# Moving the cosine and sine tables of a fused encoder layer into its modulation steps

## The chip, the cores and the metric

One core of one Trainium2 chip runs the whole layer. The metric is the device time of one execution in microseconds (us), as the median of several runs; the profile is one execution taken by the hardware profiler.

## The reference, cut to what matters

Sequence length 1024, model width 1024, one layer, float32. The rotary part of the second attention group needs the cosine and the sine of 1024 positions times 32 frequencies:

```python
mod = jax.nn.silu(c) @ ada_w + ada_b
shift, scale, gate = jnp.split(mod, 3, axis=-1)
h = _rms_norm(x, norm_g) * (1.0 + scale[:, None, :]) + shift[:, None, :]
proj = h @ w_in
dq, dk, dv, cq, ckv, kr, g = jnp.split(proj, [int(v) for v in cuts], axis=-1)
...
inv_freq = ROPE_THETA ** (-jnp.arange(half, dtype=jnp.float32) / half)
ang = positions.astype(jnp.float32)[:, :, None] * inv_freq
cos, sin = jnp.cos(ang), jnp.sin(ang)
q_pe = _rope(q_pe, cos[:, :, None, :], sin[:, :, None, :])
k_pe = jnp.broadcast_to(_rope(kr, cos, sin)[:, :, None, :], (B, S, MLA_HEADS, MLA_ROPE_DIM))
...
out = (mixed * jax.nn.silu(g)) @ w_out
return x + gate[:, None, :] * out
```

`dq`, `dk`, `dv` feed a differential attention, `cq`, `ckv`, `kr` a latent attention (MLA); both are chunk-causal.

## The kernel before, in words

The program has three phases: `prologue`, `projections` and `mixing`. Only the first and the start of the second matter here.

Products of two float32 operands are made of three matrix products each (`mm3`, lines 63 to 65): both operands are split into a rounded part and a rest, `hTh` and `hTl` for the activations, `wh` and `wl` for the weights. A raw weight tile `wraw` of 128 rows is loaded by SyncE's queue, cast to `wh` on ScalarE (line 534), and `wl = wraw - wh` is made on GpSimd or on VectorE (line 535). There are five buffers for `wraw` and eight for each of `wh` and `wl`, so the tiles of the next unit of weights are taken in as those of the last are done with.

The prologue normalizes `x`, transposes it to `xT` (eight slices `k` of 128 of the model width, two halves `b` of 512 tokens each), and then runs **modulation steps**, one for each `k`, in an order that is written out by hand for TensorE, VectorE, ScalarE and GpSimd (`manual_schedule`). While TensorE multiplies slice `k` with the MLA columns of `w_in` (448 columns) for seven of the eight tiles of 128 tokens (`step`, lines 392 to 398), the step makes the operands of slice `k + 1`:

- TensorE forms a part of `silu(c) @ ada_w` (`gemv`, `gv`, line 322), ScalarE copies it (line 324), TensorE turns it into a column (`mod`, line 330), and this comes in the middle of TensorE's step.
- VectorE makes scale and shift of the slice from it (`ab_mod`, lines 332 to 334).
- `modulated` does for each half `b`: VectorE forms `h32` (line 374, shown as `h`), ScalarE `hTh` (line 375), VectorE `hTl` from both (line 377).
- `split` casts slice `k + 2` of the weights on ScalarE (`wh`) and makes `wl` on GpSimd; `load` fetches slice `k + 4`.

In the last step VectorE does `gain_products` (lines 140 to 149) in the place of a modulation. After the steps the pool `x`, which holds the input tiles, is closed, and the pool `tmp` takes its memory. From here on a scheduler sets the order of instructions on each engine. `mla_evac` copies the seven accumulators from PSUM to `lat` (line 602 on ScalarE, line 604 on VectorE). TensorE does the eighth token tile (`u1b`) and then the unit of 512 columns for the keys `dk` (the first `u` of lines 63 to 65 with 512 columns); its tiles of results take turns in the PSUM banks that the accumulators held, and are emptied by way of `sq`, `ss`, `r` and `xn` (line 561). `mla_latent` normalizes `lat`, and `mla_weights` splits the weights that MLA needs.

`rope_tables` stands after the first `mla_latent`. It loads the positions and the frequencies through GpSimd's queue (lines 160 and 161), and makes the tables `cc` (cosine) and `sc` (sine, with sign) with 29 operations on VectorE, nearly all on 128 x 256 elements and each on the result of the one before: the angle, its reduction to one turn, a series for the sine, a series for the cosine, and four copies into the tables (lines 234 and 235). Its scratch is taken from the stage buffers of `tmp` (the tile `scr`). The tables are first read when `mla_tile` rotates `kr` on GpSimd (`rope`, lines 645 to 648), in the first token tiles of the unit `dk`.

Of the kernel before, what the change touches and what calls it, by code (L numbers as in the profile page):

```python
# [17 lines left out]
P = 128  # L18
S = 1024
D = 1024  # L20
# [25 lines left out]
GAINS = 4  # L46


class Fused:
# [101 lines left out]
    def rope_tables(self):  # L151
# [16 lines left out]
        )  # L168
        n = buf()
        stt = v.scalar_tensor_tensor  # L170

        def reduce_turns(t):
            v.tensor_scalar(n, t, MAGIC, None, op0=ALU.add)
            v.tensor_scalar(n, n, -MAGIC, None, op0=ALU.add)
            v.tensor_tensor(t, t, n, op=ALU.subtract)

        if not self.general:

            v.tensor_scalar(n, ang, 1.0 / (2.0 * math.pi), MAGIC, op0=ALU.mult, op1=ALU.add)
            v.tensor_scalar(n, n, -MAGIC, None, op0=ALU.add)  # L180
            p1 = 6.28125
            p2 = 507.0 * 2.0 ** -18
            p3 = 2.0 * math.pi - p1 - p2
            for p in (p1, p2, p3):
                stt(ang, n, -p, ang, op0=ALU.mult, op1=ALU.add)
            v.tensor_scalar(ang, ang, -4.0, 4.0, op0=ALU.max, op1=ALU.min)
        else:
# [6 lines left out]
            v.tensor_copy(hi, ang)  # L194
            v.tensor_tensor(lo, ang, hi.bitcast(F32), op=ALU.subtract)
            limbs = []
# [6 lines left out]
            for limb in reversed(limbs):  # L203
                for part in (lo, hi.bitcast(F32)):
                    v.tensor_scalar(f, part, limb, None, op0=ALU.mult)
                    reduce_turns(f)
                    reduce_turns(f)
                    if first:
                        v.tensor_copy(tot, f)
                        first = False  # L210
                    else:
                        v.tensor_tensor(tot, tot, f, op=ALU.add)
                        reduce_turns(tot)
            v.tensor_scalar(ang, tot, 2.0 * math.pi, None, op0=ALU.mult)
            parts += [hi.bitcast(F32).rearrange("p t n -> p (t n)"), f.rearrange("p t n -> p (t n)")]

        y, sh, ch = n, buf(), buf()
        stt(y, ang, 0.25, ang, op0=ALU.mult, op1=ALU.mult)

        def series(out, first, last):  # L220

            v.tensor_scalar(out, y, (-1.0) ** (last // 2) / math.factorial(last), None, op0=ALU.mult)
            for d in range(last - 2, first, -2):
                stt(out, out, (-1.0) ** (d // 2) / math.factorial(d), y, op0=ALU.add, op1=ALU.mult)

        series(sh, 1, 13)
        stt(sh, sh, 1.0, ang, op0=ALU.add, op1=ALU.mult)
        series(ch, 0, 14)
        stt(ch, ch, 1.0, sh, op0=ALU.add, op1=ALU.mult)

        stt(sh, sh, -0.5, sh, op0=ALU.mult, op1=ALU.mult)
        for h in range(2):
            sl = slice(h * 32, h * 32 + 32)
            v.tensor_scalar(self.cc[:, :, sl], sh, 1.0, None, op0=ALU.add)
            v.tensor_scalar(self.sc[:, :, sl], ch, -1.0 if h == 0 else 1.0, None, op0=ALU.mult)


    def prologue(self):
# [176 lines left out]
        rows_r = xp.tile([P, 4, P], F32, name="rows_r")  # L415
        rbc = [xp.tile([P, 512], F32, name=f"rbc{b}") for b in range(2)]
        split = lambda k: self.split_rows(unit, raws.pop(k), True)
        with self.tc.manual_schedule(engines={E.PE, E.DVE, E.Activation, E.Pool}):
# [6 lines left out]
            squares(0)  # L425
            turned(0, 0, range(6))
            squares(1)
# [1045 lines left out]
```

## Time and profile before

| | us |
|---|---|
| median of 3 runs | 679.31 (675.96 to 681.81) |
| the profiled execution | 675.18 |
| its span, first to last instruction | 673.2 |
| TensorE busy | 636.0 |
| VectorE busy | 480.0 |
| ScalarE busy | 341.3 |
| GpSimd busy | 282.5 |

In what follows PE is TensorE's matrix products, DVE VectorE, ACT ScalarE, POOL GpSimd. A row of a timeline gives the start, the length, the engine, the line, the operation and `out<-in` by the program's names; in brackets stands how long the engine was idle before it and what ended that. TensorE's products overlap one another, so the distance from start to start is what one takes. Busy time says little on an engine that waits for others by turns; what counts is the wait that ends last.

### The profile page before, as it was taken

To read this page: it belongs to the slowest core of one execution; us is meant where nothing else is said; L and a number is where in the kernel's file an instruction comes from. 1 tells how busy PE (TensorE), PEld (TensorE's weight loads), DVE (VectorE), ACT (ScalarE), POOL (GpSimd) and SP (SyncE) were. 2 spreads that over 40 slices of the span, in tenths; PEclk is the share of its full clock that TensorE was granted. 3 is DMA by queue.
4 is the path that set the end of the run, shared out by engine and by line. 5 is a ranking of instruction groups with operands and counts; after the bars stand their busy time and mean duration, and the time that the engine had idled before them with its cause. 6 is when DMAs were issued, how large, how long until landed. Compare 5 with 4: busy or idle time off the path is not lost.

```text
span 673.2 us, 11178 instructions
## 1 busy us (share of the span) xinstructions
PE 636.0 (94%) x3579; PEld 538.7 (80%) x3579; DVE 480.0 (71%) x1296; ACT 341.3 (51%) x820; POOL 282.5 (42%) x376
## 2 busy tenths in 40 slices
PE   6899998999999999989999989997999899999996
PEld 4578886878888888877888878886988788888885
DVE  5855899699987554635876867989976466367654
ACT  4433663744565344345766766877775344236200
POOL 2022415483355135304443544558655225349400
PEclk9999999999999999999999998998999999999999
DMA  9984152598657455499556385493365944514223
GB/s 323 304 203 127 41 172 58 148 286 263 185 144 217 120 162 148 133 237 291 139 151 188 98 241 132 137 289 123 95 188 169 300 144 134 148 46 126 80 111 113
DMA packets 115140, 112.97 MB, mean 168 GB/s; under 512 B 7712, under 2 KB 86614, under 8 KB 115072
## 3 DMA queue, kind: packets, MB, share of 16 engines
q1 hardware_dynamic: 114784, 112.12, 57.4%
q8 instruction: 30, 0.49, 0.3%
q14 instruction: 38, 0.31, 0.2%
q0 software_dynamic: 288, 0.05, 0.1%
HBM read 77.51 MB, written 34.62 MB: 167 GB/s over the span
## 4 chain that ended last, share of the span: by engine, by line
PE 62%; DVE 14%; DMA 11%; issue 4%; ACT 3%; POOL 3%; SPq 2%; DVEq 0%; POOLq 0%; ACTq 0%
PE lg L953 8%; PE u L63 7%; PE u L65 7%; PE u L64 7%; PE o L65 4%; PE o L63 4%; PE o L64 4%; PE pt L1019 3%; DVE p L962 3%; DMA raw<-mk_d 2%; PE acc L64 2%; PE acc L65 2%; PE acc L63 2%; PE u L392 2%; DMA dk<-dk_d 2%
## 5 line engine op out<-in xcount | busy, mean ns | idle before, releaser
L972 ACT ACTIVATE p<-p,mx 128x128 f32<-128x128 f32 (+7 forms) x96 | 74.3, 775 | 35.4 <-DVE p L967 19.2
L63 PE MATMUL u<-wh,hTh 128*128 128x512 f32 x192 | 75.8, 398 | 3.3 <-DVE xn L561 2.6
L65 PE MATMUL u<-wh,hTl 128*128 128x512 f32 x192 | 76.3, 397 | 0.0
L64 PE MATMUL u<-wl,hTh 128*128 128x512 f32 x192 | 75.7, 394 | 0.0
L962 DVE TENSOR_SCALAR_CACHE_REDUCE p<-lg 128x512 f32<-128x512 f32 (+5 forms) x96 | 52.6, 563 | 13.3 <-PE pt L1019 4.5
L953 PE MATMUL lg<-dk,dq 128*128 128x512 f32 (+2 forms) x192 | 52.2, 368 | 5.6 <-DVE p L962 3.3
L535 POOL TENSOR_TENSOR wl<-wraw,wh 128x512 fp32r<-128x512 f32 (+1 forms) x20 | 26.5, 1329 | 65.4 <-ACT wh L534 60.7
L63 PE MATMUL u<-hTh,wh 128*128 128x512 f32 x128 | 51.5, 402 | 0.0
L65 PE MATMUL u<-hTh,wl 128*128 128x512 f32 x128 | 51.0, 399 | 0.0
L64 PE MATMUL u<-hTl,wh 128*128 128x512 f32 x128 | 50.5, 394 | 0.0
L1019 PE MATMUL pt<-ident_r,p 128*128 128x128 f32 x288 | 45.9, 276 | 3.4 <-DVE pTl L1021 1.7
L63 PEld LDWEIGHTS u<-wh,hTh 128*128 128x128 f32 x192 | 36.1, 188 | 10.6 <-DVE xn L561 3.3
L65 PEld LDWEIGHTS u<-wh,hTl 128*128 128x128 f32 x192 | 36.1, 188 | 7.2 <-issue 0.4
L64 PEld LDWEIGHTS u<-wl,hTh 128*128 128x128 f32 x192 | 36.1, 188 | 6.7
L953 PEld LDWEIGHTS lg<-dk,dq 128*128 128x128 f32 x192 | 31.4, 195 | 11.3 <-DVE p L962 6.1
L1021 DVE TENSOR_TENSOR pTl<-pt,pTh 128x512 fp32r<-128x512 f32 x48 | 32.9, 688 | 10.6 <-ACT pTh L1020 10.2
L1107 POOL TENSOR_SCALAR p<-p,sm 128x128 f32<-128x128 f32 (+7 forms) x32 | 25.7, 806 | 34.7 <-DVE sm L1106 34.1
L1052 DVE SCALAR_TENSOR_TENSOR p<-p,sm,p 128x128 f32<-128x128 f32 (+7 forms) x32 | 33.1, 1040 | 9.7 <-POOL p L1051 9.7
L1019 PEld LDWEIGHTS pt<-ident_r,p 128*128 128x128 f32 x288 | 34.2, 141 | 6.4 <-DVE p L1052 2.5
L1020 ACT CAST pTh<-pt 128x512 fp32r<-128x512 f32 x48 | 27.5, 581 | 21.0 <-PE pt L1019 20.6
L1051 POOL TENSOR_SCALAR p<-p,sm 128x128 f32<-128x128 f32 (+7 forms) x32 | 25.5, 797 | 27.6 <-DVE sm L1050 10.6
L953 PE MATMUL lg<-mkh,mq 128*128 128x512 f32 (+2 forms) x96 | 34.0, 365 | 0.7 <-ACT mq L877 0.7
(321 smaller groups left out, 1913.8 us busy)
## 6 DMA issues: line engine op xcount, KB each, us to landing
wraw<-in_w_in_dram SPq DMA_DIRECT2D x40, 256.0 KB, 3.4
ada<-in_ada_w_dram SPq DMA_DIRECT2D x32, 256.0 KB, 6.6
dq<-dq_d SPq DMA_DIRECT2D x16, 512.0 KB, 6.9
xt<-in_x_dram SPq DMA_DIRECT2D x8, 512.0 KB
dk_d<-st SPq DMA_DIRECT2D x16, 256.0 KB
adag<-in_ada_w_dram SPq DMA_DIRECT2D x16, 256.0 KB
dq_d<-st SPq DMA_DIRECT2D x16, 256.0 KB, 3.1
sg_d<-sgt SPq DMA_DIRECT2D x16, 256.0 KB, 4.7
```

Of the source, the lines that this page charges most:

```text
L63: t.matmul(out, wh, xh, start=start, stop=False)
L64: t.matmul(out, wh, xl, start=False, stop=False)
L65: t.matmul(out, wl, xh, start=False, stop=stop)
L535: (nc.gpsimd if pool else nc.vector).tensor_tensor(l, raw, h.bitcast(F32), op=ALU.subtract)
L953: self.last_mm = nc.tensor.matmul(lg[:, :w], q, k, start=j == 0, stop=j == len(ops) - 1 and not add)
L962: nc.vector.tensor_scalar(o[:, :m], lg[:, :m], 1.0, mx if c0 else None, op0=ALU.mult, op1=ALU.min, accum_out=mx)
L972: nc.scalar.activation(p, p, AF.Exp, bias=mx, scale=-1.0, accum_out=sm)
L1019: nc.tensor.transpose(t[:, j * P : j * P + P], ptiles[e[1]][:, e[0] * P : e[0] * P + P], self.ident)
L1020: nc.scalar.copy(h[:, lo:512], t[:, lo:512])
L1021: nc.vector.tensor_tensor(l[:, lo:512], t[:, lo:512], h[:, lo:512].bitcast(F32), op=ALU.subtract)
L1052: v.scalar_tensor_tensor(pp[0], pp[0], sm[:, 0:1], pp[1], op0=ALU.mult, op1=ALU.add)
L1107: nc.gpsimd.tensor_scalar(p, p, sm[:, 0:1], 0.0, op0=ALU.mult, op1=ALU.add)
```

## The change

`rope_tables` becomes a generator that yields after each load and each VectorE operation. Its scratch is now a tile `rt` of the pool `x` and, behind it, input tiles `xt` that have been used; its tables lie in the pool `w2`, which lives through the projections. The two loads are issued on GpSimd after the first transposes. In each modulation step, after both `modulated` and ahead of `split`, four operations are taken from the generator, and what is left after the last step. The call behind the first `mla_latent` goes.

```diff
+ROPE_OPS = 4
...
-    def rope_tables(self):
+    def rope_tables(self, parts):
...
-        self.cc = self.tmp.tile([P, NT, 64], F32, name="cc")
-        self.sc = self.tmp.tile([P, NT, 64], F32, name="sc")
-        parts = [t[:, h * 256 : h * 256 + 256] for t in [self.scratch(tag) for tag in ("mst", "mst", "mst", "st")] for h in range(2)]
+        self.cc = self.w2.tile([P, NT, 64], F32, name="cc")
+        self.sc = self.w2.tile([P, NT, 64], F32, name="sc")
         raw = parts.pop()
...
         nc.gpsimd.dma_start(posi, i["positions"].rearrange("o (t p) -> p (o t)", p=P))
+        yield
         nc.gpsimd.dma_start(inv, i["cst"][:, 640:672])
+        yield
         v.tensor_copy(posf, posi)
+        yield
...
+        rt = xp.tile([P, D], F32, name="rt")
...
             squares(0)
+            rope = self.rope_tables([t[:, 256 * h : 256 * h + 256] for t in (rt, *xs) for h in range(4)][::-1])
             turned(0, 0, range(6))
+            for _ in range(2):
+                next(rope)
             squares(1)
...
                 if more:
                     for b in range(2):
                         modulated(b, k + 1)
+                for _ in range(ROPE_OPS):
+                    next(rope, None)
                 if k + 2 < KT:
                     split(k + 2)
                 if k + 4 < KT:
                     load(k + 4)
                 if k == GAINS:
                     self.load_gains(junk[0])
+            for _ in rope:
+                pass
         xctx.close()
...
         self.mla_latent(0)
-        self.rope_tables()
```

On VectorE, from one modulation to the next (the fifth and the sixth slice), there stood before the two halves' `h` and `hTl` and the next `ab_mod`:

```order
L374 SCALAR_TENSOR_TENSOR h_667<-xTk,ab_mod,rbc_180 128x512
L377 SCALAR_TENSOR_TENSOR hTl<-h_667,ab_mod,hTh 128x512
L374 SCALAR_TENSOR_TENSOR h_672<-xTk,ab_mod,rbc_181 128x512
L377 SCALAR_TENSOR_TENSOR hTl<-h_672,ab_mod,hTh 128x512
L332 TENSOR_SCALAR ab_mod<-mod,cols 128x1
```

At the same place there stands now, with the lines of the changed program (`rt` is the scratch of the tables):

```order
L399 SCALAR_TENSOR_TENSOR h_684<-xTk,ab_mod,rbc_181 128x512
L402 SCALAR_TENSOR_TENSOR hTl<-h_684,ab_mod,hTh 128x512
L399 SCALAR_TENSOR_TENSOR h_689<-xTk,ab_mod,rbc_182 128x512
L402 SCALAR_TENSOR_TENSOR hTl<-h_689,ab_mod,hTh 128x512
L243 SCALAR_TENSOR_TENSOR rt<-rt 128x256 x3
L247 SCALAR_TENSOR_TENSOR rt<-rt 128x256
L357 TENSOR_SCALAR ab_mod<-mod,cols 128x1
```

Four operations of the tables have come between the last `hTl` of a slice and the `ab_mod` of the next. There are five such groups ahead of an `ab_mod`, and a sixth ahead of the gain products.

On ScalarE, behind the last modulation, there stood before the copies of four accumulators to `lat`, and the first cast of the next unit's weights (`wh`) behind them:

```order
L375 ACTIVATE hTh<-h_786,ab_mod 128x512
L147 ACTIVATE junk<-junk 128x2
L602 COPY lat<-u_301 128x448
L602 COPY lat<-u_307 128x448
L602 COPY lat<-u_413 128x448
L602 COPY lat<-u_425 128x448
L612 ACTIVATE sq,ss<-lat 128x256
L613 ACTIVATE sq,ss<-lat 128x128
L612 ACTIVATE sq,ss<-lat 128x256
L534 CAST wh<-wraw 128x512
```

Now there stands:

```order
L400 ACTIVATE hTh<-h_811,ab_mod 128x512
L566 CAST wh<-wraw 128x512
L148 ACTIVATE junk<-junk 128x2
L566 CAST wh<-wraw 128x512 x5
L634 COPY lat<-u_306 128x448
L634 COPY lat<-u_312 128x448
L634 COPY lat<-u_418 128x448
L634 COPY lat<-u_430 128x448
```

Six casts have moved ahead of the four copies. On VectorE, the end of the tables and three `wl` stand likewise ahead of the three copies to `lat`:

```order
L147 TENSOR_REDUCE junk<-junk 128x2
L567 TENSOR_TENSOR wl<-wraw,wh 128x512
L149 TENSOR_TENSOR nlam<-junk 128x1
L150 TENSOR_SCALAR nlam<-nlam 128x1
L253 SCALAR_TENSOR_TENSOR rt<-rt 128x256
L567 TENSOR_TENSOR wl<-wraw,wh 128x512
L257 TENSOR_SCALAR cc<-rt 128x8x32
L259 TENSOR_SCALAR sc<-xt 128x8x32
L257 TENSOR_SCALAR cc<-rt 128x8x32
L259 TENSOR_SCALAR sc<-xt 128x8x32
L567 TENSOR_TENSOR wl<-wraw,wh 128x512
L872 MEMSET small 32x128
```

The copies to `lat` on VectorE follow this piece directly; before, they followed `nlam`.

## Rows read from the trace of the kernel before

**Rows 1.** The page: the span, and busy time of TensorE and VectorE
```profile
span 673.2 us, 11178 instructions
...
PE 636.0 (94%) x3579; PEld 538.7 (80%) x3579; DVE 480.0 (71%) x1296; ACT 341.3 (51%) x820; POOL 282.5 (42%) x376
```

**Rows 2.** Busy time by stretch: modulation steps, then the next 33 us
```profile
core 0: us, PE busy (x) PEld busy (x) DVE busy (x) ACT busy (x) POOL busy (x), PEclk, DMA share, GB/s
30.00:72.00 42.00, 41.05 (x272) 32.80 (x271) 24.42 (x58) 15.17 (x29) 7.52 (x6) 1.00 0.62 158
72.00:105.00 33.00, 31.02 (x143) 25.86 (x141) 32.60 (x116) 22.21 (x82) 11.28 (x17) 1.00 0.41 117
```

**Rows 3.** TensorE's waits from 72 to 300 us: total, times, longest
```profile
PE u L63 <- DVE xn L561: 2.6, 2, 2.2
PE kn L65 <- DVE cl L672: 1.4, 1, 1.4
```

**Rows 4.** VectorE's timeline of one modulation step
```profile
41.28 0.22 DVE L332 TENSOR_SCALAR ab_mod<-mod,cols 128x1 f32<-128x1 f32 x1 [0.98 <-PE mod L330]
41.53 0.16 DVE L333 TENSOR_TENSOR ab_mod<-ab_mod,cols 128x1 f32<-128x1 f32 x1
41.61 0.15 DVE L334 TENSOR_TENSOR ab_mod<-mod,cols 128x1 f32<-128x1 f32 x1
...
43.27 0.75 DVE L377 SCALAR_TENSOR_TENSOR hTl<-h,ab_mod,hTh 128x512 fp32r<-128x512 f32 x1 [0.79 <-ACT hTh L375]
...
45.48 0.75 DVE L377 SCALAR_TENSOR_TENSOR hTl<-h,ab_mod,hTh 128x512 fp32r<-128x512 f32 x1 [0.79 <-ACT hTh L375]
47.18 0.22 DVE L332 TENSOR_SCALAR ab_mod<-mod,cols 128x1 f32<-128x1 f32 x1 [0.95 <-PE mod L330]
```

**Rows 5.** Groups of VectorE, 74 to 104 us, by form: busy, mean ns, idle
```profile
L224 DVE SCALAR_TENSOR_TENSOR scr<-scr 128x256 f32<-128x256 f32 x11 | 4.5, 410 | 0.0
...
L234 DVE TENSOR_SCALAR cc<-scr 128x256 f32<-128x256 f32 x2 | 0.5, 284 | 0.0
...
L162 DVE CAST scr<-scr 128x8 f32<-128x8 int32 x1 | 0.2, 172 | 0.3 <-DMA scr<-in_positions_dram 0.3
```

**Rows 6.** GpSimd's timeline: its first `wl`, a step's, two behind the steps
```profile
13.38 1.14 POOL L535 TENSOR_TENSOR wl<-wraw,wh 128x448 fp32r<-128x448 f32 x1 [9.90 <-ACT wh L534]
...
45.98 1.25 POOL L535 TENSOR_TENSOR wl<-wraw,wh 128x448 fp32r<-128x448 f32 x1 [4.67 <-DMA ada<-in_ada_w_dram]
...
75.94 1.30 POOL L535 TENSOR_TENSOR wl<-wraw,wh 128x512 fp32r<-128x512 f32 x1
77.56 1.39 POOL L535 TENSOR_TENSOR wl<-wraw,wh 128x512 fp32r<-128x512 f32 x1 [0.33 <-ACT wh L534]
```

**Rows 7.** The tile `wraw`, 30 to 100 us: minimum, median, maximum
```profile
L535 DVE TENSOR_TENSOR wl<-wraw,wh x4: 679/682/1880, 75.9 to 86.1; 128x512 fp32r<-128x512 f32 x4
...
DMA to landing us min/median/max: 2.9/3.5/4.0
```

**Rows 8.** VectorE's timeline beside the last two rows of GpSimd
```profile
75.91 1.88 DVE L535 TENSOR_TENSOR wl<-wraw,wh 128x512 fp32r<-128x512 f32 x1
77.72 1.38 DVE L179 TENSOR_SCALAR scr<-scr 128x256 f32<-128x256 f32 x1
```

**Rows 9.** ScalarE's timeline at the end of the steps
```profile
68.42 0.72 ACT L375 ACTIVATE hTh<-h,ab_mod 128x512 fp32r<-128x512 f32 x1 [1.48 <-DVE h L374]
...
71.51 1.84 ACT L602 COPY lat<-u 128x448 f32<-128x448 f32 x4 [0.35 <-PE u L398]
...
74.32 0.63 ACT L534 CAST wh<-wraw 128x512 fp32r<-128x512 f32 x1
```

**Rows 10.** TensorE's timeline: last step, `u1b`, the next unit, its stall
```profile
69.47 0.47 PE L392 MATMUL u<-wh,hTh 128*128 128x448 f32 x1
...
72.21 0.37 PE L63 MATMUL u1b<-wh,hTh 128*128 128x448 f32 x1
...
77.07 1.07 PE L63 MATMUL u<-wh,hTh 128*128 128x512 f32 x4
...
105.22 0.50 PE L63 MATMUL u<-wh,hTh 128*128 128x512 f32 x1 [2.20 <-DVE xn L561]
```

More of the change, by code (lines that the diff above doesn't have):

```diff
@@ L168, in rope_tables @@
         )
+        yield
         n = buf()
@@ L173, in reduce_turns @@
             v.tensor_scalar(n, t, MAGIC, None, op0=ALU.add)
+            yield
             v.tensor_scalar(n, n, -MAGIC, None, op0=ALU.add)
+            yield
             v.tensor_tensor(t, t, n, op=ALU.subtract)
+            yield
         if not self.general:
             v.tensor_scalar(n, ang, 1.0 / (2.0 * math.pi), MAGIC, op0=ALU.mult, op1=ALU.add)
+            yield
             v.tensor_scalar(n, n, -MAGIC, None, op0=ALU.add)
+            yield
             p1 = 6.28125
@@ L185, in rope_tables @@
                 stt(ang, n, -p, ang, op0=ALU.mult, op1=ALU.add)
+                yield
             v.tensor_scalar(ang, ang, -4.0, 4.0, op0=ALU.max, op1=ALU.min)
+            yield
         else:
@@ L194, in rope_tables @@
             v.tensor_copy(hi, ang)
+            yield
             v.tensor_tensor(lo, ang, hi.bitcast(F32), op=ALU.subtract)
+            yield
             limbs = []
@@ L205, in rope_tables @@
                     v.tensor_scalar(f, part, limb, None, op0=ALU.mult)
-                    reduce_turns(f)
-                    reduce_turns(f)
+                    yield
+                    yield from reduce_turns(f)
+                    yield from reduce_turns(f)
                     if first:
                         v.tensor_copy(tot, f)
+                        yield
                         first = False
@@ L212, in rope_tables @@
                         v.tensor_tensor(tot, tot, f, op=ALU.add)
-                        reduce_turns(tot)
+                        yield
+                        yield from reduce_turns(tot)
             v.tensor_scalar(ang, tot, 2.0 * math.pi, None, op0=ALU.mult)
+            yield
             parts += [hi.bitcast(F32).rearrange("p t n -> p (t n)"), f.rearrange("p t n -> p (t n)")]
@@ L218, in rope_tables @@
         stt(y, ang, 0.25, ang, op0=ALU.mult, op1=ALU.mult)
+        yield
         def series(out, first, last):
             v.tensor_scalar(out, y, (-1.0) ** (last // 2) / math.factorial(last), None, op0=ALU.mult)
+            yield
             for d in range(last - 2, first, -2):
                 stt(out, out, (-1.0) ** (d // 2) / math.factorial(d), y, op0=ALU.add, op1=ALU.mult)
-        series(sh, 1, 13)
+                yield
+        yield from series(sh, 1, 13)
         stt(sh, sh, 1.0, ang, op0=ALU.add, op1=ALU.mult)
-        series(ch, 0, 14)
+        yield
+        yield from series(ch, 0, 14)
         stt(ch, ch, 1.0, sh, op0=ALU.add, op1=ALU.mult)
+        yield
         stt(sh, sh, -0.5, sh, op0=ALU.mult, op1=ALU.mult)
+        yield
         for h in range(2):
@@ L234, in rope_tables @@
             v.tensor_scalar(self.cc[:, :, sl], sh, 1.0, None, op0=ALU.add)
+            yield
             v.tensor_scalar(self.sc[:, :, sl], ch, -1.0 if h == 0 else 1.0, None, op0=ALU.mult)
+            yield
     def prologue(self):
```

## The prediction

> **What bounds the kernel now.** I read the page first: TensorE is busy for 636.0 of 673.2 us, VectorE for 480.0 [rows 1]. The profiled execution took 675.2 us, 2.0 us around its span, and 4.1 us under the median of 679.31 us; three runs of one kernel lie 5.85 us apart, so about 1% (6.8 us) is what a measurement tells from no change. Next the table of stretches: in the modulation steps (30 to 72 us) VectorE works 24.42 of 42 us, in the next 33 us it works 32.60, and that second stretch is where 29 operations for the tables stand now [rows 2]. That makes the move look free at its goal and useful at its source. So two questions decide: what TensorE loses to VectorE at the source, and whether VectorE's idle time in the steps is of use at the place in the order where the operations now stand.
>
> First question, from the list of TensorE's waits between 72 and 300 us: 2.6 us for `xn` (one wait of 2.2 us) and 1.4 us for `cl`, and little else [rows 3]. So much can come back, and not the 8 to 12 us that 29 operations of 0.28 to 0.41 us take [rows 5].
>
> Second question, from VectorE's timeline of one step [rows 4]. The step runs from `ab_mod` at 41.28 to the next `ab_mod` at 47.18, 5.90 us. Its idle time is in three pieces: two of 0.79 us, in which VectorE waits for ScalarE's `hTh`, and 0.95 us, in which it waits for TensorE's `mod`. The new operations stand behind the last `hTl` and ahead of the next `ab_mod`: the first two pieces they can't use, since VectorE takes its instructions in order. So four operations have 0.95 us, and what runs over delays the next `ab_mod`.
>
> **Four operations in a step.** The same operations in the trace take 0.41 us (scalar_tensor_tensor) and 0.28 us (tensor_scalar), the cast 0.17 [rows 5]. They form a chain. An operation that needs the one before begins 0.03 us after its end (`ab_mod` at 41.28, 0.22 long, the next at 41.53), one that doesn't begins 0.08 us before it (41.53, 0.16 long, the next at 41.61) [rows 4]. The Trainium skill ("VectorE: DVE Perf Modes", The DRAIN you can't avoid) says otherwise: chaining with a semaphore after every operation costs no more than with one at the end. By it each group would be 3 x 0.11 us shorter, and the whole sum 1.7 us less; the rows at 41.53 and 41.61 speak against it, and I go by the rows.
>
> Undisturbed, four chained operations end at 46.15 + 0.41 + 3 x 0.44 = 47.88, and the next `ab_mod` begins at 47.80 in place of 47.18: +0.62 us.
>
> **The collision.** They aren't undisturbed. GpSimd's `wl` of the same step runs from 45.98 to 47.23, and there is one in each of the steps that matter here [rows 6]. Further on in the trace one sees what happens to a VectorE operation on SBUF that comes up during such a one: the 128x512 `wl` on VectorE, 0.68 us alone [rows 7], took 1.88 and ended 0.55 after GpSimd's; a tensor_scalar of the table's own code, 0.28 alone, took 1.38 and ended 0.15 after GpSimd's [rows 6, 8]. It stands still until GpSimd is done. (The Trainium skill, "SBUF — State Buffer", Who interferes with whom, has it as an exclusive lock that goes to whichever engine issues first; it speaks against the place chosen here.) Whether GpSimd holds back the first of the four or, if that one slips in behind `hTl`, the second, the sum is the same: of the group three chained operations lie behind 47.23, and a rest of the first of 0.28. So 47.23 + 0.28 + 3 x 0.44 = 48.83, the next `ab_mod` at 48.75: +1.57 us. Five groups lie ahead of `ab_mod`s, and each has a GpSimd `wl` beside it:
> - group 1 (cast, product, two tensor_scalars): 47.23 + 0.10 + 0.45 + 0.32 + 0.31, +1.15
> - groups 2 and 3 (three scalar_tensor_tensor, one tensor_scalar): +1.45 each
> - group 4 (four scalar_tensor_tensor): +1.57
> - group 5 (tensor_scalar first, whose rest is 0.15): +1.44
>
> ScalarE's `wh` and GpSimd's `wl` of a step hang on VectorE's `h` of the same step, so they move with it and collide again: the delays add up, to 7.1 us at the last `ab_mod`. TensorE has slack, but it is used once, not per step. In the last step `hTh` of the second half ends at 68.42 + 0.72 = 69.14 [rows 9] and TensorE reads it at 69.47 [rows 10]: 0.33 us. So TensorE leaves the steps **6.7 us late**. Without the collision the five groups give 0.14 + 0.50 + 0.50 + 0.62 + 0.50 = 2.26, and TensorE 1.9 us: that is the lower bound of this term, 7.1 the upper.
>
> **The start of the next unit.** Now ScalarE copies the accumulators to `lat` at 71.51, as soon as the steps end, and casts the next weights from 74.32 [rows 9]; TensorE's product for the eighth token tile, `u1b` (72.21 to 77.07, 4.86 us) covers both, and the unit begins at 77.07 without a wait [rows 10]. In the new order six casts stand ahead of the four copies, and the tables' end stands ahead of VectorE's copies. Counted from the start of `u1b`: the first cast waits until `u1b` has read that buffer (three of its 24 products and their tail, 0.8), 0.63 long, 1.4; VectorE's `wl` of it 0.68, 2.1; only then can the sixth raw tile be loaded, 2.9 at least to land [rows 7], 5.0; its cast 5.6; the first copy 1.84 / 4 = 0.46 later, 6.1. TensorE could go at 4.86: 1.2 us idle. Besides, `lat` lies where the tables' scratch lay, so it waits for the tables' last operations, and these now stand among three VectorE `wl` while GpSimd runs up to three of 1.30 us [rows 6]: one or two of them in the way put the tables' end at 6.7 to 7.9 and the copy at 7.2 to 8.4, so 2.3 to 3.6 us idle. I take **2.3**, the bound with one in the way; ends 1.2 and 3.6.
>
> **What comes back.** The 29 operations, the stall of VectorE behind GpSimd among them, leave the full stretch. The wait of 2.2 us at 105.22 should go [rows 10]: VectorE then reaches `xn` without most of those 8 to 12 us in front of it. Of the other waits for VectorE up to 300 us (0.4 and 1.4) I count half: in sum **3.1**; bounds 1 (the wait only moves) and 4.0 (both groups of [rows 3] gone).
>
> **Costed at nothing.** The two loads from GpSimd's queue come in the 9.90 us that GpSimd is idle ahead of its first `wl` at 13.38 [rows 6], and are wanted in the steps only. The tables lie in another pool for the whole projection, which makes nothing wait in the lists of either order. From some 75 us on the scheduler's order differs on every engine; I can't price that, and leave 1.5 us on either side.
>
> **Sum.** 6.7 + 2.3 - 3.1 = **+5.9 us**: 675.2 becomes 681.1 for an execution like the profiled one, and 679.3 becomes 685.2 on the median.
>
> **Rivals.**
> 1. *No collision* (chance 0.17). If GpSimd's `wl` and the four operations pass one another, 1.9 + 1.2 - 3.1 = 0.0: 679.3, no change. For it: `hTl` at 45.48 and `wl` at 45.98 overlap in the trace already and neither is visibly longer. Against it: [rows 6, 8].
> 2. *The steps hide it all* (0.05). If the four operations fit into the idle pieces, the steps cost nothing, the unit begins on time and the waits of [rows 3] go: -4.0, 675.3, faster. The point that decides is whether the groups' chain is under 0.95 us per step; the durations in [rows 5] say 1.6. For it speaks only the busy share, 24.42 of 42.
> 3. *The new order after the steps costs more* (0.23). If the first unit's weights come late behind both the tables and GpSimd, 3.6 at the start, 1.5 more inside the unit, and only 1.0 comes back: 6.7 + 3.6 + 1.5 - 1.0 = +10.8, 690.1.
> 4. *The tables don't really move*: 25 of the 29 operations stand within the steps or right behind them, and the order shows them there; no chance is given to it.
>
> **How the numbers follow.** The forecast, +5.9 with its bounds (6.7 + 1.2 - 4.0 to 7.1 + 3.6 - 1.0, and 1.5 for the order: +2.4 to +11.2), has 0.55. Its time lies under the 1% bound by 0.9 us only, so of its chance 0.20 lies above the bound, and of rival 3 0.21; rival 1 and the rest lie within it. Faster by over 1% needs more than all waits up to 300 us and gets 0.02. So slower 0.41, within 1% 0.57. The range goes from rival 1 less 1.3 us for the spread of runs (678) to rival 3 (691).
>
> **What the profile would show.** Right: distances from `ab_mod` to `ab_mod` of 7.0 to 7.5 us in five steps, TensorE idle in each of the later ones, waiting for `hTh`; the operation behind `hTl` or the one after it over 1 us long; `u1b` near 79 us; TensorE idle some 2 us before the next unit; no 2.2 us wait for `xn` afterwards. Wrong: steps that stay at 5.9 us (rival 2) or come to 6.4 (rival 1), or a TensorE that waits for `wl` inside the first unit (rival 3).

## The result: 1.6% slower, and the profile after

The changed kernel takes 687.41 us (median of 4 runs, 687.24 to 689.90). The runs of the kernel before beside it have a median of 678.89 us (675.96 to 681.81). The ratio is 1.016, 95% interval 1.0121 to 1.0198. Timed again beside the last experiments it was 687.59 us, ratio 1.0188 (1.0133 to 1.0244). The kernel before ran 71 times more in the course of the experiments, with a median of 675.7 us, so the true difference is nearer to 11 or 12 us than to 8. Five of these 71, the second profiled one below (682.62 us) among them, lie more than 1.5% over the fastest beside them, so its column, the first `again`, shows one end of the scatter and not a typical execution.

The page of the changed kernel, to be read against [rows 1]:

```profile
span 685.6 us, 11168 instructions
...
PE 637.8 (93%) x3579; PEld 539.8 (79%) x3579; DVE 489.5 (71%) x1296; ACT 343.6 (50%) x820; POOL 285.2 (42%) x376
```

TensorE works as long as before (637.8 against 636.0 us) and the span is 12.4 us longer: the loss is idle time. VectorE is busy for 9.5 us more with the same number of instructions (1296), so some operations are drawn out. The five collisions in the steps, one of which is shown next, make about half of it (0.94 us each).

VectorE's timeline of one modulation step, against [rows 4]:

```profile
45.27 0.21 DVE L357 TENSOR_SCALAR ab_mod<-mod,cols 128x1 f32<-128x1 f32 x1
...
47.26 0.75 DVE L402 SCALAR_TENSOR_TENSOR hTl<-h,ab_mod,hTh 128x512 fp32r<-128x512 f32 x1 [0.79 <-ACT hTh L400]
...
49.46 0.75 DVE L402 SCALAR_TENSOR_TENSOR hTl<-h,ab_mod,hTh 128x512 fp32r<-128x512 f32 x1 [0.79 <-ACT hTh L400]
50.13 2.28 DVE L194 SCALAR_TENSOR_TENSOR rt<-rt 128x256 f32<-128x256 f32 x3
52.44 0.29 DVE L196 TENSOR_SCALAR rt<-rt 128x256 f32<-128x256 f32 x1
52.65 0.21 DVE L357 TENSOR_SCALAR ab_mod<-mod,cols 128x1 f32<-128x1 f32 x1
```

GpSimd's timeline beside it, against [rows 6]:

```profile
49.96 1.25 POOL L567 TENSOR_TENSOR wl<-wraw,wh 128x448 fp32r<-128x448 f32 x1 [5.75 <-ACT wh L566]
```

Three operations of 0.41 us take 2.28 us, since the first stands still until GpSimd's `wl` ends at 51.21. The idle 0.95 us ahead of `ab_mod` is gone. The two gaps of 0.79 us are still there, unused. From `ab_mod` to `ab_mod` the step takes 7.38 us, where it took 5.90.

TensorE's timeline at the places that mark the stages, and at its long waits, against [rows 10]:

```profile
81.87 0.36 PE L64 MATMUL u1b<-wh,hTh 128*128 128x448 f32 x1
...
89.85 0.50 PE L64 MATMUL u<-wh,hTh 128*128 128x512 f32 x1 [2.96 <-ACT lat L634]
...
276.42 0.39 PE L64 MATMUL u<-hTh,wh 128*128 128x512 f32 x1
...
452.97 0.80 PE L985 MATMUL lg<-dk,dq 128*128 128x256 f32 x2 [3.70 <-DVE p L994]
...
544.03 0.55 PE L64 MATMUL acc<-pTh,vh 128*128 128x256 f32 x1 [4.03 <-DVE sg L1147]
```

The third row is the first product of the units whose operands are exchanged (`hTh` first). Before, it stands at 268.01. Together with the first `ab_mod` and `u1b` it parts the run into four stages that can be compared although the scheduler's order differs. The table also has a second profiled execution of either kernel (last experiments), in us:

```
                              before  again   after  again
first ab_mod of the steps      29.77  31.65   32.68  33.10
from it to u1b                 42.44  42.42   49.19  49.20
u1b to the exchanged product  195.80 195.70  194.55 196.11
the rest of the span          405.19 410.83  409.18 408.29
span                          673.2  680.6   685.6  686.7
```

Only the second row differs by much more than two executions of one program do: +6.8 us. The first differs by 1.9 us between two executions of the kernel before, the last by 5.6. Against the first execution of the kernel before, though, the last row is 3 to 4 us longer in both of the changed kernel, and the section on the order after the steps shows that this much is real.

Two views remain. ScalarE's timeline at the start of the next unit, against [rows 9]:

```profile
86.75 0.62 ACT L566 CAST wh<-wraw 128x512 fp32r<-128x512 f32 x1 [0.98 <-DMA wraw<-in_w_in_dram]
89.27 1.84 ACT L634 COPY lat<-u 128x448 f32<-128x448 f32 x4 [1.90 <-DVE sc L259]
```

TensorE's waits from 81 to 277 us (total, times, longest), against [rows 3]:

```profile
PE u L64 <- ACT lat L634: 3.0, 1, 3.0
PE u L64 <- DVE xn L593: 0.4, 1, 0.4
PE kn L66 <- DVE cl L704: 0.3, 1, 0.3
```

The copies to `lat` wait for the tables' last operation (`sc`), and TensorE waits for them, 2.96 us. In return the waits for `xn` (2.6) and `cl` (1.4) are down to 0.7 together.

### The profile page after: what moved, and what is told of

Its sections match the earlier page's. It is cut to its first block, busy times and chain, and to the rows that moved or that the text cites. A ratio compares the mean times of both kernels' runs of the same rounds, so it can differ in the third digit from the quotient of the medians.

```text
span 685.6 us, 11168 instructions
## 1 busy us (share of the span) xinstructions
PE 637.8 (93%) x3579; PEld 539.8 (79%) x3579; DVE 489.5 (71%) x1296; ACT 343.6 (50%) x820; POOL 285.2 (42%) x376
## 4 chain that ended last, share of the span: by engine, by line
PE 61%; DVE 14%; DMA 10%; ACT 5%; issue 4%; POOL 2%; SPq 2%; POOLq 0%; DVEq 0%; ACTq 0%
PE u L64 8%; PE u L66 8%; PE u L65 8%; PE lg L985 7%; PE o L64 4%; PE o L66 4%; PE o L65 4%; PE pt L1051 3%; PE acc L64 2%; DVE p L994 2%; DMA raw<-dv_d 2%; PE acc L66 2%; PE acc L65 2%; ACT hTh L400 2%; DVE h L399 2%
## 5 line engine op out<-in xcount | busy, mean ns | idle before, releaser
L1004 ACT ACTIVATE p<-p,mx 128x384 f32<-128x384 f32 (+7 forms) x96 | 74.4, 776 | 29.7 <-DVE p L999 18.0
L1083 POOL TENSOR_SCALAR p<-p,sm 128x128 f32<-128x128 f32 (+7 forms) x32 | 27.2, 850 | 39.6 <-ACT sgt L832 16.1
L1084 DVE SCALAR_TENSOR_TENSOR p<-p,sm,p 128x128 f32<-128x128 f32 (+7 forms) x32 | 35.8, 1121 | 9.7 <-POOL p L1083 9.5
L985 PEld LDWEIGHTS lg<-dk,dq 128*128 128x128 f32 x192 | 30.6, 190 | 14.5 <-DVE p L994 10.0
L1139 POOL TENSOR_SCALAR p<-p,sm 128x128 f32<-128x128 f32 (+7 forms) x32 | 25.4, 796 | 29.6 <-DVE sm L1138 28.6
```

The lines of the kernel that those rows point to most:

```text
L985: self.last_mm = nc.tensor.matmul(lg[:, :w], q, k, start=j == 0, stop=j == len(ops) - 1 and not add)
L1004: nc.scalar.activation(p, p, AF.Exp, bias=mx, scale=-1.0, accum_out=sm)
L1083: nc.gpsimd.tensor_scalar(pp[1], pp[1], sm[:, 1:2], 0.0, op0=ALU.mult, op1=ALU.add)
L1084: v.scalar_tensor_tensor(pp[0], pp[0], sm[:, 0:1], pp[1], op0=ALU.mult, op1=ALU.add)
```

## Experiments

### What lengthens the steps: the collision with GpSimd's `wl`

**GpSimd's `wl` taken out of the steps**

This version leaves out the low halves of five rows of weights; TensorE multiplies by another row's low half in their place.

```diff
                 if k + 2 < KT:
-                    split(k + 2)
+                    h = self.weight_pair()[0][:, :448]
+                    a.copy(h, raws.pop(k + 2))
+                    unit[0].append(h)
+                    unit[1].append(unit[1][2])
```

> The changed kernel without GpSimd's five wl of the modulation steps (the low halves of five weight rows are left out; TensorE multiplies by another row's low half in their place, so as many products run). The table operations stand where the change has them. Theory (the operation behind hTl stands still until GpSimd's wl is done): with no wl there, four chained operations end 0.14 to 0.62 us after the moment at which ab_mod could go, so the distances from ab_mod to ab_mod are 6.05, 6.4, 6.4, 6.5, 6.4 us in place of 7.01, 7.38, 7.38, 7.51, 7.38, no table operation takes over 0.5 us, u1b comes 4.5 to 5 us earlier than 81.9, and the time is 3 to 5 us under the changed kernel's 687.4. Rival (four chained operations at this place cost 1.5 us by themselves): distances of 7.0 us and more, time unchanged.

VectorE's timeline of the same step without `wl`:

```profile
43.81 0.21 DVE L357 TENSOR_SCALAR ab_mod<-mod,cols 128x1 f32<-128x1 f32 x1
...
48.00 0.75 DVE L402 SCALAR_TENSOR_TENSOR hTl<-h,ab_mod,hTh 128x512 fp32r<-128x512 f32 x1 [0.79 <-ACT hTh L400]
48.67 1.34 DVE L194 SCALAR_TENSOR_TENSOR rt<-rt 128x256 f32<-128x256 f32 x3
50.05 0.29 DVE L196 TENSOR_SCALAR rt<-rt 128x256 f32<-128x256 f32 x1
50.26 0.21 DVE L357 TENSOR_SCALAR ab_mod<-mod,cols 128x1 f32<-128x1 f32 x1
```

The three operations take 1.34 us in place of 2.28. The distances are 6.07, 6.45, 6.45, 6.58, 6.45 us, within 0.08 of the expectation, and `u1b` begins at 76.67, 5.2 earlier. Median 677.24 us, ratio to the kernel before 1.0009 (0.9969 to 1.0049), 10 us under the changed kernel and so more than the 3 to 5 us expected. From the first `ab_mod` to `u1b` it takes 44.5 us, 4.7 less than the changed kernel. The rest lies outside the steps, where the scheduler's order is another one too (see the order after the steps). The collision is shown: some 0.94 us of each step.

**The same operations in the gaps of 0.79 us, two in each**

```diff
-ROPE_OPS = 4
+GAP_OPS = 2, 2
...
             a.activation(self.hTh[:, k, sl], h32, AF.Identity, bias=shift)
+            for _ in range(GAP_OPS[b] if k else 0):
+                next(self.ropes, None)
...
-                for _ in range(ROPE_OPS):
-                    next(rope, None)
```

> The changed kernel with one thing different: the table operations stand not behind the last hTl of a step but two at a time between h and hTl of each half, where VectorE waits 0.79 us for hTh and GpSimd has no wl beside it; 28 of the 29 fit into the seven pairs of halves. Theory (what cost was the place, which meets GpSimd's wl and then holds ab_mod): two chained operations take 0.72 to 0.85 us, so 0 to 0.1 us per half runs over, the distances from ab_mod to ab_mod are 5.9 to 6.2 us in place of 7.0 to 7.5, no operation of the tables takes over 1 us, the ninth-tile product u1b starts near 76 us (72.2 + 2.9 for the early loads + about 1), and the time is 6 to 9 us under the changed kernel: 678.5 to 681.5. Rival (the steps have no room on VectorE wherever the operations stand): distances of 7 us and a time within 1.5 us of 687.4.

VectorE's timeline of a step of this version:

```profile
44.59 0.22 DVE L357 TENSOR_SCALAR ab_mod<-mod,cols 128x1 f32<-128x1 f32 x1 [0.98 <-PE mod L355]
...
45.04 0.75 DVE L399 SCALAR_TENSOR_TENSOR h<-xTk,ab_mod,rbc 128x512 f32<-128x512 f32 x1
45.71 0.42 DVE L235 SCALAR_TENSOR_TENSOR rt<-rt 128x256 f32<-128x256 f32 x1
46.16 0.29 DVE L240 TENSOR_SCALAR rt<-rt 128x256 f32<-128x256 f32 x1
46.59 0.75 DVE L404 SCALAR_TENSOR_TENSOR hTl<-h,ab_mod,hTh 128x512 fp32r<-128x512 f32 x1
47.26 0.75 DVE L399 SCALAR_TENSOR_TENSOR h<-xTk,ab_mod,rbc 128x512 f32<-128x512 f32 x1
47.92 0.88 DVE L243 SCALAR_TENSOR_TENSOR rt<-rt 128x256 f32<-128x256 f32 x2
48.80 0.75 DVE L404 SCALAR_TENSOR_TENSOR hTl<-h,ab_mod,hTh 128x512 fp32r<-128x512 f32 x1
50.53 0.22 DVE L357 TENSOR_SCALAR ab_mod<-mod,cols 128x1 f32<-128x1 f32 x1 [0.98 <-PE mod L355]
```

The distance is 5.93 to 5.94 us, as before the change, with four operations more in the step: they stand where VectorE waited for `hTh`, and the 0.98 us ahead of `ab_mod` stay. Median 677.05 us, ratio 1.0028 (0.9995 to 1.0061), 10 us under the changed kernel, where 6 to 9 were expected; 6.7 us of this are the steps, which take 42.5 us again from the first `ab_mod` to `u1b`. The steps had room for all of it; the place decided.

**All four in the first gap**

The edit is shown against the version with two in each gap.

```diff
-GAP_OPS = 2, 2
+GAP_OPS = 4, 0
```

> The changed kernel with one thing different: the same four chained operations of a step stand together between h and hTl of the first half only. The group of 1.6 to 1.8 us overruns that gap of 0.79 us by 0.9, but GpSimd is idle there and VectorE has 0.95 us to spare ahead of the next ab_mod. Theory (collision costs, not the chain): no table operation is drawn out beyond 0.5 us. What is late by 0.9 are hTl of the first half and all of the second half, and with it GpSimd's wl, which then lies over the next ab_mod: its second operation reads from SBUF only and may be held until wl ends, so distances of 6.0 us without and about 6.7 with that. Time 2 to 8 us under the changed kernel. Rival (the four chained operations cost 1.5 us per step wherever they stand in the order): distances of 7.4 us and a time as the changed kernel's.

No operation was drawn out (three took 1.34 us, the fourth 0.29). The distances are 6.28 to 6.42 us, between the two values expected; neither of the reasons given is in the rows. The 0.64 us ahead of `ab_mod` is still a wait for TensorE's `mod`, and among TensorE's waits from 32 to 77 us stands `mod` for ScalarE's `gemv`, 1.8 us in three times. So the step seems to be set by the loop of `hTh`, `gemv`, `mod` and `ab_mod`, 0.4 us longer than before; that wasn't tried by itself. Median 678.48 us, ratio 1.0028 (0.9998 to 1.0057).

### The start of the next unit

**The tables' scratch in the tables' own memory**

```diff
...
+        if not self.general:
+            parts = [t[:, :, x : x + 32] for x, t in ((0, self.sc), (0, self.cc), (32, self.sc), (32, self.cc))]
...
-        for h in range(2):
+        for h in (1, 0):
...
```

> The changed kernel with the tables' scratch inside the two tables' own memory in place of the first tiles' memory, so that lat, which later lies over the first tiles, no longer waits for the tables' last operations. Operations, their number and their places in the steps stay. Theory: the steps stay at 7.0 to 7.5 us; ScalarE's copy to lat is no longer released by sc, and TensorE's idle time at the start of the next unit falls from 2.96 us to 0 to 1.2 (what the raw tile of the sixth cast costs). The time falls by 1.5 to 3 us, to about 685. Rival (the copies are late because of the casts ahead of them, not of the tables' end): idle time stays at 2.5 to 3 us, no gain. In either case the order after the steps is drawn up anew, which may move the time by some us later on.

ScalarE's and TensorE's rows at that place:

```profile
82.45 1.40 ACT L636 COPY lat<-u 128x448 f32<-128x448 f32 x3
```

```profile
84.52 0.36 PE L66 MATMUL u1b<-wh,hTl 128*128 128x448 f32 x1
84.72 0.39 PE L64 MATMUL u<-wh,hTh 128*128 128x512 f32 x1
```

The unit begins right behind `u1b`; the 2.96 us are gone, so the memory shared with the tables' scratch was their cause. Yet from `u1b` to the exchanged product it takes 194.52 us, as the changed kernel does (194.55): waits for `cl` (1.4), `vst` (1.4) and `st` (0.6) have taken its place. Median 687.14 us, ratio 1.0159 (1.0109 to 1.0209). The wait was real and worth nothing: TensorE starts this stage earlier and waits later in it.

### The first 30 us

**The loads at 29 us, changed kernel**

```diff
-            for _ in range(2):
-                next(rope)
             squares(1)
...
             split(2)
             load(4)
+            for _ in range(2):
+                next(rope)
```

> The changed kernel with one thing different: the two small loads (positions and frequencies) go out on GpSimd's queue after the second weight split and the fifth step's loads, about 29 us into the program, in place of 3.4 us. Theory: the two early loads hold back SyncE's issues of the modulation weights and tiles and so make the first 30 us 2.9 us longer. Then the first ab_mod of the steps comes at 29.8 us (as before the change) and not at 32.7, the distances in the steps stay at 7.0 to 7.5 us, and the time is 2 to 3.5 us under the changed kernel, about 684.5. Rival (the first 30 us differ from execution to execution whatever the loads do): the first ab_mod stays anywhere between 29.8 and 32.7, and the time stays within 1 us of 687.4.

First `ab_mod` at 30.38, steps unchanged (7.01 to 7.51 us), median 685.99 us, ratio 1.0115 (1.0079 to 1.0151). The loads came out of GpSimd's queue only behind the third `wl`, after 35 us. The lists of TensorE, VectorE and ScalarE are the changed kernel's here, row for row.

**The loads early, kernel before**

```diff
...
-        nc.gpsimd.dma_start(posi, i["positions"].rearrange("o (t p) -> p (o t)", p=P))
-        nc.gpsimd.dma_start(inv, i["cst"][:, 640:672])
...
             turned(0, 0, range(6))
+            nc.gpsimd.dma_start(rt[:, 0:NT].bitcast(I32), i["positions"].rearrange("o (t p) -> p (o t)", p=P))
+            nc.gpsimd.dma_start(rt[:, 2 * NT : 2 * NT + 32], i["cst"][:, 640:672])
             squares(1)
```

> The kernel before with one thing different: only the two small loads move to where the change has them (GpSimd's queue, among the first tiles' loads), into a small tile of their own; the table operations stay after the projection. Theory: the first ab_mod of the steps comes 2.9 us later, at 32.7 in place of 29.8, all else shifts by as much, and the time is 2 to 3.5 us over the kernel before (about 682). Rival (it is not the loads): first ab_mod at 29.8 and no change of time beyond 1 us.

First `ab_mod` at 31.00, so +1.2 and not +2.9; median 681.82 us, ratio 1.0075 (1.0049 to 1.0101), +5.2. Theory and rival are both missed: the start explains a quarter of the loss. The scheduler's order after the steps differs too (and the cast of the positions has moved ahead of the steps), with the waits of 3.7 us for `p` and 4.2 for `sg` that the changed kernel has.

**The loads at 25 us, changed kernel, no row of TensorE, VectorE or ScalarE moved; and either kernel profiled once more**

```diff
-            for _ in range(2):
-                next(rope)
             squares(1)
...
             split(1)
+            for _ in range(2):
+                next(rope)
```

> The changed kernel with the two loads issued behind GpSimd's second wl (about 25 us) in place of 3.4 us. The lists of TensorE, VectorE and ScalarE are the changed kernel's, row for row, so unlike in the earlier runs no later order differs. Theory (the early loads hold back the first 30 us): first ab_mod 1 to 2.9 us earlier than in the changed kernel and a median 1 to 3 us under it. Rival (the start differs between executions only): medians within 1 us of one another.

> The changed kernel unaltered, timed again beside the next one, and profiled a second time to see what differs between executions of one program. Theory (the distances in the steps are set by the order, the first 30 us and the granted clock after 270 us by the execution): distances 7.01, 7.38, 7.38, 7.51, 7.38 again to within 0.05 us, the first ab_mod anywhere from 30.5 to 33; time 686 to 688.

> The kernel before unaltered, one more profiled execution. Theory (the start and the clock differ from execution to execution): distances of 5.58 to 5.93 us again, first ab_mod between 29.5 and 32, and the stretch from the first spilled product to the end 398 to 404 us depending on the granted clock (398.5 in the execution shown). Rival (the kernel before starts at 29.8 always): 29.8 within 0.2.

First `ab_mod` at 30.00 with the loads late, 33.10 in the changed kernel again, and 31.65 in the kernel before again: its rival (29.8 always) falls. Medians 685.98 us with the loads at 25 us (ratio 1.0195, 1.0139 to 1.0250) and 687.59 us in the changed kernel (1.0188, 1.0133 to 1.0244); the medians lie 1.6 us apart, the ratios the other way round, and the intervals over one another. SyncE's issues in the three profiles, first the changed kernel, then the loads at 25 us, then the kernel before again:

```profile
2.60 4.80 SPq L312 DMA_DIRECT2D ada<-in_ada_w_dram  x4
```

```profile
2.60 3.43 SPq L312 DMA_DIRECT2D ada<-in_ada_w_dram  x4
```

```profile
2.60 4.37 SPq L287 DMA_DIRECT2D ada<-in_ada_w_dram  x4
```

The four issues of the first modulation weights take 4.80 us beside the early loads and 3.43 without them, but 4.37 in an execution of the kernel before. Over all profiles, eight with early loads and six without, these issues take 4.28 to 4.97 us with them and 3.38 to 4.37 without, the DMA moves 5.52 to 5.61 MB in the first 18 us against 5.74 to 5.82, and the first `ab_mod` comes at 30.6 to 33.1 us (median 32.2) against 29.8 to 31.7 (median 30.2). So other transfers do fall behind beside the early loads. These cost the start some 2 us, with as much scatter between executions; how much of it reaches the kernel's time, 1.6 us by the medians, isn't settled.

### The order after the steps

**Five operations in a step**

```diff
-ROPE_OPS = 4
+ROPE_OPS = 5
```

> The changed kernel with five table operations per step in place of four (one number changed), so the steps get longer and the tables end with the steps. The order that the scheduler draws up after the steps is another one here: from the first logits on, TensorE's list stands close to that of the kernel before (436 rows of difference; the changed kernel has 1178). Theory (the later order is worth 3 to 5 us by itself): distances from ab_mod to ab_mod of 7.45 to 7.85 us, 2 us more in sum than in the changed kernel, so u1b some 2 us later from the same start; no wait for lat at the unit's start (3.0 saved); no wait of 3.7 us for p and none of 4 us for sg among TensorE's waits; time 680 to 684 although the steps are longer. Rival (the order after the steps makes no difference): u1b later by 2, the unit's start 3 earlier, and a time of about 686.5 with the waits for p and sg as in the changed kernel.

Distances 7.47 to 7.97 us and `u1b` at 82.28, from a first `ab_mod` at 30.88: the steps are 2.2 longer, as expected. No wait for `lat`, and TensorE's waits show neither long one:

```profile
PE pt L1051 <- DVE p L1084: 3.0, 2, 2.1
PE lg L985 <- DVE p L994: 2.8, 4, 1.4
...
PE acc L64 <- DVE sg L1147: 1.1, 1, 1.1
```

But the median is 686.41 us, ratio 1.0151 (1.0104 to 1.0197): 2 us over the expectation and on the rival's 686.5. Both of these count 3.0 us as saved at the unit's start, though, and the run with the scratch showed this saving to be worth nothing. Without it the rival names 687.4 + 2.2 = 689.6 us and the theory 3 to 5 less, and 686.41 lies 3.2 under the rival. Alone this is no proof, since its interval and that of the changed kernel timed again (1.0133 to 1.0244) lie over one another.

All runs together settle more. A version has both long waits or neither, and its steps are longer by a known amount. With this taken off its median, the rest of the program can be compared (us; the table has the versions of the next section too):

| version | longest wait for `p` | for `sg` | median | steps longer by | median less that |
|---|---|---|---|---|---|
| changed kernel | 3.7 | 4.0 | 687.4 | 6.8 | 680.6 |
| the same again | 3.7 | 3.8 | 687.6 | 6.8 | 680.8 |
| loads at 29 us | 3.7 | 3.0 | 686.0 | 6.8 | 679.2 |
| loads at 25 us | 3.7 | 3.1 | 686.0 | 6.8 | 679.2 |
| scratch in the tables | 3.7 | 4.7 | 687.1 | 6.8 | 680.3 |
| gaps, loads at 29 us | 3.7 | 3.2 | 684.9 | 4.8 | 680.1 |
| kernel before, loads early | 3.7 | 4.2 | 681.8 | 0.0 | 681.8 |
| five operations | 1.4 | 1.1 | 686.4 | 9.0 | 677.4 |
| without `wl` | 1.4 | 0.6 | 677.2 | 2.1 | 675.1 |
| four in the first gap | 1.4 | 1.2 | 678.5 | 2.3 | 676.2 |
| two in each gap | 1.4 | none | 677.0 | 0.0 | 677.0 |
| gaps, loads at 25 us, scratch | 1.4 | 0.6 | 673.2 | 0.0 | 673.2 |
| kernel before (71 executions) | 1.4 | 0.8 | 675.7 | 0.0 | 675.7 |

The seven rows with the two waits lie at 679.2 to 681.8, the six without at 673.2 to 677.4, some 4 us lower; the kernel before, timed beside each of the groups of runs, lay at 674.9 to 676.6 (678.9 in the four executions beside the first row). Both groups have early and late loads, and both have the tables' operations in the old place, in the gaps and behind `hTl`. So an order with these two waits takes some 4 us more than one without. That the waits alone cost it, and not what else differs between these orders, wasn't tried. How the first of them comes about stands in VectorE's timeline of the changed kernel:

```profile
449.85 1.73 DVE L1084 SCALAR_TENSOR_TENSOR p<-p,sm,p 128x1024 f32<-128x1024 f32 x1 [3.29 <-POOL p L1083]
451.50 1.21 DVE L910 TENSOR_TENSOR mq<-raw,mq 128x512 fp32r<-128x512 f32 x1
452.63 0.28 DVE L994 TENSOR_SCALAR_CACHE_REDUCE p<-lg 128x128 f32<-128x128 f32 x1
```

VectorE waits 3.29 us for GpSimd's part of `p`, and the operation that TensorE waits for stands behind it. In the kernel before, VectorE waits 1.33 us at the same operation.

### A version that is faster than both

**In the gaps, from the second step on, loads at 29 us**

```diff
-            for _ in range(GAP_OPS[b] if k else 0):
+            for _ in range(GAP_OPS[b] if k > 1 else 0):
```

> Two operations in each gap between h and hTl, as in the second experiment of this kind, but from the second step on, and the two loads issued about 29 us into the program, behind the first tiles and the fifth step's loads; 24 operations are in the gaps and five behind the last step. Theory: distances of 5.93 us as before the change, the first ab_mod at about 30 us in place of 33.1 with the early loads, and a time 1 to 3 us under the 677.05 of the version with early loads, 674 to 676. That would be 0 to 0.4% under the kernel before. Rival (the start is not set by the loads, or the five operations left over hold up the next unit): 677 or more.

The edit is shown against the version with two in each gap; the loads stand where the first experiment on them has them. A miss. The loads were issued behind GpSimd's third `wl`, and VectorE stood for them in front of `hTl`. GpSimd's and VectorE's timelines:

```profile
35.88 0.95 POOL L160 DMA_DIRECT2D rt<-in_positions_dram  x1
```

```profile
39.91 0.17 DVE L164 CAST rt<-rt 128x8 f32<-128x8 int32 x1 [3.13 <-DMA rt<-in_positions_dram]
40.86 0.42 DVE L168 TENSOR_TENSOR rt<-rt 128x256 f32<-128x256 f32 x1 [0.78 <-DMA rt<-in_cst_dram]
```

Two steps took 9.21 and 7.43 us. Median 684.87 us, ratio 1.013 (1.0082 to 1.0179).

**The same, loads behind GpSimd's second `wl`, scratch in the tables' memory**

The edit joins the gaps from the second step on, the loads behind `split(1)`, and the scratch of above.

> Two operations in each gap between h and hTl from the second step on, the scratch inside the tables' own memory, and the two loads on GpSimd's queue right behind its second wl, so issued at about 24.8 us and landed by 33, ahead of the first gap that needs them at 36. By the list TensorE's later order is close to that of the kernel before (440 rows of difference). Theory: the first ab_mod of the steps at 29.8 to 30.6 us, distances of 5.93 us, u1b at 72.2 to 73, no wait at the unit's start, and what the full stretch after the steps gives back comes on top: 672.5 to 675.5 us, 0 to 0.6% under the kernel before. Rival (the loads cost at any place): first ab_mod or the third step late by over 1 us, and 676 to 678.

The page of this version:

```profile
span 674.3 us, 11190 instructions
...
PE 637.8 (95%) x3579; PEld 542.0 (80%) x3579; DVE 483.1 (72%) x1296; ACT 342.6 (51%) x820; POOL 281.2 (42%) x376
```

Its waits of TensorE from 75 to 275 us, all of them:

```profile
PE kt L606 <- DVE st L621: 0.6, 1, 0.6
PE kn L66 <- DVE cl L706: 0.2, 1, 0.2
```

Distances 5.93 and 5.94 us; 191.37 us from `u1b` to the exchanged product, 4.4 less than before the change; 0.8 us of waits there in place of the 4.0 of [rows 3]. The first `ab_mod` came at 31.63 in this execution, a miss of 1 us by the scatter told above. Median 673.24 us (12 runs) against 675.25, ratio 0.996 (0.9928 to 0.9992). It is faster than the changed kernel by 14 us and than the kernel before by 0.4%, with an interval that just leaves out 1. Since it is the best of several versions tried, so small a margin over the kernel before is weak evidence; the 14 us aren't.

## Why the prediction was right and where it wasn't

The time came out at 687.4 us, 2.2 over the forecast of 685.2 and inside the range. The difference did not: +5.9 us was forecast, 8.5 (beside the first runs) to 12.7 (beside the last) were measured, so the outcome is "slower by over 1%", to which the prediction gave 0.41, and not its likelier "within 1%". The two agree in time only because the three runs it started from (median 679.31) lie 3.6 us over the median of the 71 later ones; that is luck.

- **Four operations in a step, and the collision: right.** Forecast distances 7.05, 7.35, 7.35, 7.47, 7.34; measured 7.01, 7.38, 7.38, 7.51, 7.38. TensorE leaves the steps 6.8 us late by this term, 6.7 were forecast. The bound without a collision, 1.9, is what the kernel without `wl` shows: 76.67 - 32.16 - 42.44 = 2.07. The Trainium skill ("SBUF — State Buffer", Who interferes with whom) has the lock go to whichever engine issues first. In the step shown GpSimd's `wl` began at 49.96 and the VectorE operation 0.17 later, so the rows agree; in a step without the collision the price is 0.94 us less. By the Trainium skill's other rule ("VectorE: DVE Perf Modes", The DRAIN you can't avoid) a semaphore after each operation of a chain would cost nothing extra. Three chained operations of 0.41 take 1.34 us without `wl`, 0.11 over their sum, so the sum by the rows stands.
- **What TensorE would wait for: half right.** Its idle time was put down to `hTh`. From 33 to 82 us it waits 4.5 us for `gemv` on its way to `mod`, and 1.5 for `hTh`. The loop is the same; the link at which it shows isn't.
- **The start of the next unit: mechanism right, worth wrong.** 2.3 us were forecast and 2.96 stand there, released by the tables' end as told. But with that wait taken away the stage took as long. So the step "2.3 idle and 3.1 back" went wrong by treating the two as separate terms. Together they were -0.8; the stage gave -1.25, and +0.4 in the second pair of executions.
- **What comes back: right in size.** The waits of [rows 3] fell from 4.0 to 0.7 us, 3.3 less against 3.1 forecast.
- **Costed at nothing, the two loads: this step failed.** They were held to be harmless in an idle queue. By fourteen profiles other transfers fall behind beside them, and they cost some 2 us of the first 30 (1.6 us of the time by the medians of two kernels with the same lists of TensorE, VectorE and ScalarE), though not through GpSimd's own work: SyncE's issues beside them took longer.
- **Costed at nothing, the order from 75 us on (1.5 either way): too narrow.** An order with the waits of 3.70 and 4.03 us takes some 4 us more than one without. With 6.8 in the steps and about 1.5 at the start this makes 12 us, and 11 to 12 were measured. What of the 4 us are the waits themselves stays open, and so does what in the change made the scheduler choose such an order. The granted clock is no further term, since it is in these medians already: the changed kernel's ten executions have a median of 0.986, those of the kernel before 0.990, and in the changed kernel it falls in both waits (last section).
- **Rivals.** No collision (1) falls with the step's timeline. What spoke for it is seen again there, `hTl` running to 50.21 beside a `wl` begun at 49.96: not the operation under way was held in this step, but the next. "The steps hide it all" (2) holds for another place in the order, not for this one. Rival 3 named a sum of +10.8, close to what was measured, but by other means: neither 1.5 us inside the unit nor a return of only 1.0 is in the rows. That the new order costs more is true, but behind the first unit, where it wasn't looked for.

## What to carry to other kernels

Idle time of an engine is of use only where the moved instruction stands in that engine's order, and only if no engine that locks it out works there at that moment: the table operations cost 6.8 us behind the last `hTl` of a step and nothing in the two gaps ahead of it. A wait that one can name isn't yet a gain; follow what waits next. Where a scheduler sets the order behind an edit, its new order is a term of its own, here some 4 us beside 6.8. And before a difference of 1% is taken apart, profile the same program more than twice: here a second profile of the kernel before, 7 us over its median, hid those 4 us, and only the medians of all versions side by side showed them.

## What the runs showed of the hardware that was not expected

The kernel's time goes with the granted clock of the execution. Of the 66 executions of the kernel before that lie within 1.5% of the fastest beside them, the 7 with 0.984 or less have a median of 678.4 us, and the 12 with 0.994 or more one of 672.4. Which of the two brings about the other isn't told apart by this. In the changed kernel the clock falls inside the two long waits (columns: stretch, length, busy time of TensorE, weight load, VectorE, ScalarE, GpSimd, granted clock, DMA share, GB/s):

```profile
450.00:451.00 1.00, 0.00 (x0) 0.00 (x0) 1.00 (x1) 0.47 (x2) 0.83 (x5) 0.68 0.81 248
451.00:452.00 1.00, 0.00 (x0) 0.00 (x0) 1.00 (x2) 1.00 (x3) 0.99 (x1) 0.50 1.00 401
456.00:457.00 1.00, 1.00 (x7) 1.00 (x7) 1.00 (x3) 1.00 (x5) 0.00 (x0) 0.50 0.85 209
457.00:458.00 1.00, 1.00 (x9) 1.00 (x9) 0.54 (x5) 0.52 (x3) 0.33 (x1) 0.90 1.07 258
458.00:459.00 1.00, 1.00 (x9) 1.00 (x8) 0.66 (x2) 0.83 (x2) 0.59 (x3) 1.00 0.80 287
540.00:550.00 10.00, 5.97 (x18) 5.02 (x19) 3.76 (x7) 3.34 (x6) 2.66 (x4) 0.66 1.02 283
```

The levels are 2.4 GHz (1.00) and 1.2 GHz (0.50). TensorE stands still from 449.27; the clock falls in the stretch from 450 to 451 and is back at 458, so the products from 452.97 to about 457 run at the lower level. Those of 128x256 follow one another at 0.21 us there and at 0.12 behind 459. The other wait, from 540.00 to 544.03, looks alike: a mean of 0.66 between the levels is two thirds of its stretch at the lower one. So each of these waits costs its length and then some of the products that follow it: some 2 us behind the first, an estimate from the 4 us at half the clock.
